# A decoder layer on one core: shift's first sum in quarters, eight groups of columns first, x scaled by GpSimd, the first products in the order of their parts

## The chip, the cores and the metric

The kernel runs on one core of one Trainium2 chip. Its time is device microseconds of one execution. TensorE (PE in the profile) multiplies, and its weight loads (PEld) run beside the products; VectorE (DVE), ScalarE (ACT) and GpSimd (POOL) compute on tiles of 128 partitions; SyncE (SP) issues most of the transfers.

## The reference

One layer of a decoder for 256 positions of width 2048. A conditioning vector c gives shift, scale and gate, and the normalised x is scaled and shifted by them into h. One wide product h W_in feeds two branches, a gated DeltaNet with 32 value heads and an mLSTM with 8 heads. Their outputs are projected, gated, added, projected once more, normalised, and added to x.

```python
shift, scale, gate = jnp.split(jax.nn.silu(c) @ w_ada + b_ada, 3, axis=-1)
h = rms_norm(x, norm_pre_w) * (1.0 + scale[:, None]) + shift[:, None]
proj = h @ w_in
...
merged = jax.nn.sigmoid(gate_a) * y_a + jax.nn.sigmoid(gate_b) * y_b
out = merged @ w_out
return x + gate[:, None] * rms_norm(out, norm_post_w)
```

All inputs are float32.

## The kernel before, in words

**Products in three parts.** Both operands of a product are split into a rounded part and the rest: `split` (L168) makes `hi` with a copy on ScalarE and `lo` = source - hi on VectorE or GpSimd. `mm3` (L221) then issues hi x hi, hi x lo and lo x hi into one PSUM tile. For weights, `prep_w` (L184) splits 1024 columns at a time into `whi` and `wlo`, four buffers each. `split_w` (L174) gives a share of the `wlo` to GpSimd: a counter that starts at -3072 columns and grows by 0.8 of each piece.

**The order of work is written out by hand.** The program is emitted in one order, and each engine works through its own instructions in that order. `Stream` (L63) loads units of weights over SyncE's queue (three buffers of 1 MB), prepares their pieces up to `ahead` pieces before they are used, and uses them. After each used piece `Side.step` (L45) advances the generators of the two branches by one step, up to their next `yield`; `wait(n)` (L605) yields n times. A step is thus the time of one piece.

**How h comes about.** h has 16 chunks of 128 of its 2048 columns (index k). Shift and scale of a chunk are two sums over the 2048 columns of a 1 MB row block of w_ada (`ar`) with silu(c). silu(c) as a row (`crow`) is spread over the 128 partitions by four products of one row into the PSUM tile `csil` (L282). A sum is one VectorE instruction over 2048 columns with an accumulator (L355). x is loaded (`xs`), its squares are summed (L293, L294), the root is taken as a power on GpSimd (`pow_`, L218), `x_scale` (L300) scales two chunks by it on ScalarE, and `x_turn` (L304) transposes them on TensorE and copies them back. `h_chunk` (L327) makes shift `sh` and scale `s1` on ScalarE from the sums, `hf` from both (L333), and splits hf into `h_hi` and `h_lo`.

**The start.** While w_ada comes in, 14 groups of 512 columns of W_in are multiplied in parts: BLOCKS (L340) lists which groups take which chunks k, and between which positions the w_ada units (`ada_units`, L349) are put among them. Six groups (EARLY, NE = 6) begin with chunk 0 alone. Each block's result is copied to SBUF (`part`, L413 and L415) or added to it (L411). `jtile` (L215) hands out four PSUM tiles in turn for these products and the transposes of x, so a tile's next user waits until it has been copied.

**Later.** After the start come eight periods of the DeltaNet branch. Each ends in `base_inverse` (L712), which adds `gdn_stage2` (L764) to the generators; stage 2 begins with the products `mp` (L781) on `ycmp` (L752), and after the products `mz` (L816) and their copy into x0 (L817) comes `pa` (L828). In the last period (zg = 7) nothing holds stage 2 back, as L760 does in the others. Then come four mLSTM units, `mlstm(m)` (L1009), whose `v_after` copies two PSUM tiles into `vt` (L1017), then the projections (`py`) and the last product.

## Time and profile before

| What | Value |
|---|---|
| median of 3 runs | 1606.68 us (1604.88 to 1608.56) |
| the profiled execution, its time | 1603.88 us |
| the profiled execution, its span | 1601.9 us |
| HBM read over the span | 354.40 MB |
| transfers, mean over the span | 232 GB/s |

The span runs from the first to the last instruction of the program. In the rows of the timeline the first number is the start in us from the span's start, the second the busy time, then engine, line, operation, and the tiles as out<-in; in brackets stands how long the engine had been idle and what ended it. In the rows of the stretches each engine has its busy us and, in brackets, its instructions. In the groups the numbers after the bar are busy us, mean ns of one instruction, and the engine's idle time before them.

### The profile page before, as it was taken

To read this page: it belongs to the slowest core of one execution; us is meant where nothing else is said; L and a number is where in the kernel's file an instruction comes from. 1 tells how busy PE (TensorE), PEld (TensorE's weight loads), DVE (VectorE), ACT (ScalarE), POOL (GpSimd) and SP (SyncE) were. 2 spreads that over 40 slices of the span, in tenths; PEclk is the share of its full clock that TensorE was granted. 3 is DMA by queue.
4 is the path that set the end of the run, shared out by engine and by line. 5 is a ranking of instruction groups with operands and counts; after the bars stand their busy time and mean duration, and the time that the engine had idled before them with its cause. 6 is when DMAs were issued, how large, how long until landed. Compare 5 with 4: busy or idle time off the path is not lost.

```text
span 1601.9 us, 25461 instructions
## 1 busy us (share of the span) xinstructions
PE 1577.8 (98%) x9844; PEld 1388.1 (87%) x9844; DVE 1150.1 (72%) x1801; ACT 941.0 (59%) x1503; POOL 236.7 (15%) x193
## 2 busy tenths in 40 slices
...
GB/s 375 339 406 335 279 274 195 289 238 191 170 203 175 205 148 204 164 193 169 193 169 195 149 197 176 187 214 247 290 308 305 227 249 284 283 246 244 200 273 113
DMA packets 96261, 372.37 MB, mean 232 GB/s; under 512 B 26262, under 2 KB 46214, under 8 KB 58252
## 3 DMA queue, kind: packets, MB, share of 16 engines
...
HBM read 354.40 MB, written 16.31 MB: 231 GB/s over the span
## 4 chain that ended last, share of the span: by engine, by line
PE 79%; issue 13%; DMA 3%; DVE 2%; ACT 2%; POOL 1%; SPq 0%; DVEq 0%; POOLq 0%; ACTq 0%
PE pn L223 35%; PE pt L223 28%; PE py L223 8%; DMA raw<-in_dram 1%; POOL mg L1196 1%; PE psa L223 1%; ACT whi L169 1%; DVE wlo L170 1%; DMA ya<-o_dr 1%; DMA ar<-in_dram 1%; PE mz L816 0%; PE mq L807 0%; PE pa L828 0%; PE po L856 0%; PE po L857 0%
## 5 line engine op out<-in xcount | busy, mean ns | idle before, releaser
L170 DVE TENSOR_TENSOR wlo<-raw,whi 128x1024 fp32r<-128x1024 f32 x454 | 561.5, 1245 | 253.9 <-ACT whi L169 248.8
L169 ACT CAST whi<-raw 128x1024 fp32r<-128x1024 f32 (+1 forms) x517 | 533.0, 1046 | 327.1 <-PE pn L223 148.1
L223 PE MATMUL pt<-h_hi,whi 128*128 128x256 f32 x1280 | 367.8, 287 | 0.0
L223 PE MATMUL pt<-h_hi,wlo 128*128 128x256 f32 x1280 | 362.0, 283 | 0.0
L223 PE MATMUL pt<-h_lo,whi 128*128 128x256 f32 x1280 | 362.0, 283 | 0.0
L223 PE MATMUL pn<-whi,h_hi 128*128 128x512 f32 x896 | 353.9, 395 | 6.6 <-ACT whi L169 5.7
L223 PE MATMUL pn<-wlo,h_hi 128*128 128x512 f32 x896 | 350.0, 391 | 1.1 <-POOL wlo L170 0.6
L223 PE MATMUL pn<-whi,h_lo 128*128 128x512 f32 x896 | 349.8, 390 | 0.0
L223 PEld LDWEIGHTS pt<-h_hi,whi 128*128 128x128 f32 x1280 | 245.3, 192 | 1.4
L223 PEld LDWEIGHTS pt<-h_lo,whi 128*128 128x128 f32 x1280 | 245.4, 192 | 0.3
L223 PEld LDWEIGHTS pt<-h_hi,wlo 128*128 128x128 f32 x1280 | 245.2, 192 | 0.0
L223 PEld LDWEIGHTS pn<-whi,h_hi 128*128 128x128 f32 x896 | 168.8, 188 | 42.5 <-ACT whi L169 6.1
L223 PEld LDWEIGHTS pn<-wlo,h_hi 128*128 128x128 f32 x896 | 168.8, 188 | 36.0 <-DVE wlo L170 1.3
L223 PEld LDWEIGHTS pn<-whi,h_lo 128*128 128x128 f32 x896 | 168.6, 188 | 35.3
L170 POOL TENSOR_TENSOR wlo<-raw,whi 128x1024 fp32r<-128x1024 f32 (+1 forms) x63 | 146.3, 2332 | 67.1 <-ACT whi L169 64.9
L223 PE MATMUL py<-whi,yhi 128*128 128x512 f32 x384 | 150.6, 392 | 0.7 <-ACT vt L1017 0.7
L223 PE MATMUL py<-whi,ylo 128*128 128x512 f32 x384 | 149.6, 390 | 0.0
L223 PE MATMUL py<-wlo,yhi 128*128 128x512 f32 x384 | 149.4, 389 | 0.0
L411 DVE TENSOR_TENSOR part<-pn,part 128x512 f32<-128x512 f32 x112 | 73.7, 685 | 52.6 <-PE pn L223 52.6
L169 ACT CAST yhi<-ya 128x512 fp32r<-128x512 f32 x48 | 29.9, 622 | 130.9 <-PE py L223 127.4
L170 DVE TENSOR_TENSOR ylo<-ya,yhi 128x512 fp32r<-128x512 f32 x48 | 33.2, 692 | 86.7 <-ACT yhi L169 78.7
L593 DVE SCALAR_TENSOR_TENSOR qs<-pt,gcv,qs 128x255 f32<-128x255 f32 (+2 forms) x192 | 92.2, 480 | 4.6
...
## 6 DMA issues: line engine op xcount, KB each, us to landing
raw<-in_dram SPq DMA_DIRECT2D x259, 1024.0 KB
ar<-in_dram SPq DMA_DIRECT2D x32, 1024.0 KB
...
```

What stands on the lines that cost most here:

```text
L169: A.copy(hi, src)
L170: (eng or V).tensor_tensor(lo, src, hi.bitcast(F32), op=ALU.subtract)
L223: T.matmul(ps, l, r, start=start and i == 0, stop=stop and i == 2, skip_group_check=True)
L411: V.tensor_tensor(part[g][:, b], ps[b], part[g][:, b], op=ALU.add)
L593: V.scalar_tensor_tensor(dst[:, n, sh:], src[:, 0:S - sh], taps(n, 3 - sh), dst[:, n, sh:], op0=ALU.mult, op1=ALU.add)
L1196: G.tensor_tensor(mcols(b, hf, cg), mcols(b, hf, cg), s_, op=ALU.add)
```

## The change

- **Loads.** c_row goes out on ScalarE's queue into a buffer of the w_ada ring. The first row block of w_ada (shift of chunk 0) is loaded ahead of x, the second (its scale) behind x in three column parts. The constants `bat`, `npre` and `ident` are loaded over GpSimd's queue. c as a column (`ct`) and its Silu move to the late constants.
- **Chunk 0.** Its sums leave the stream of units. The new `first_chunk` runs in place of the first piece's `prep_w`: shift's sum in four quarters, three of them before the squares of x, scale's sum in three parts, each added into `s1` at once; the mean of the squares is put together on GpSimd. The first `whi` is cast on VectorE. hf is read straight from the PSUM tile of the transposes.
- **keep_busy.** Products of a tile of zeros into the PSUM tile `zps`, three of 512 columns behind csil and two of 256 behind the first transposes.
- **First products.** `use_first` issues the twelve products of the first two groups by part: h_hi x whi, h_lo x whi, h_hi x wlo.
- **Blocks.** Eight groups begin with chunk 0 (NE = 8), with other places for the w_ada units; the stream starts with `ahead` at 1. All copies of b = 1 in the first block are VectorE's.
- **Who does what.** `x_scale` on GpSimd except for the first two chunks; `sh` and `s1` on VectorE; GpSimd's share of `wlo` starts at -1024.
- **Late.** For the last period one more step before stage 2 and one more before pa. In the last mLSTM unit the second copy into `vt` is VectorE's.

```diff
--- before.py
+++ after.py
@@ -169,7 +169,8 @@
         A.copy(hi, src)
         (eng or V).tensor_tensor(lo, src, hi.bitcast(F32), op=ALU.subtract)
 
-    share = [-3072.0, START_SHARE]
+    share = [-1024.0, START_SHARE]
+    begin = []
 
     def split_w(src, hi, lo):
 
@@ -185,6 +186,9 @@
         n = min(1024, width - h * 1024)
         hi = wp.tile([P, 1024], F32R, name="whi", tag="whi", bufs=4)
         lo = wp.tile([P, 1024], F32R, name="wlo", tag="wlo", bufs=4)
+        if begin:
+            begin.pop()(raw[:, 0:n], hi, lo)
+            return hi, lo
         split_w(raw[:, h * 1024:h * 1024 + n], hi[:, 0:n], lo[:, 0:n])
         return hi, lo
 
@@ -226,9 +230,8 @@
     bp = x0 = y0 = None
 
 
...
@@ -268,76 +271,133 @@
 
     pcs = ExitStack()
     csil = pcs.enter_context(tc.tile_pool(name="pcs", bufs=1, space=PSUM)).tile([P, D], F32, name="csil")
-    crow = [part[4 + i].rearrange("p b c -> p (b c)")[0:1] for i in range(2)]
-    for i in range(2):
-        SP.dma_start(crow[i], c_row[:, i * 1024:(i + 1) * 1024])
+
...
+    crow = ada_tile()[0:1]
+    A.dma_start(crow, c_row)
+    ar0, ar1 = load_ada(w_ada[0]), ada_tile()
     for b in range(2):
         SP.dma_start(xs[:, b], x[b * P:(b + 1) * P])
-    SP.dma_start(ident, consts[:, 0:128])
-    bat = const("bat", b_ada_t, [P, 32])
-    npre = const("npre", npre_t, [P, KC])
+    bat = cp.tile([P, 32], F32, name="bat")
+    npre = cp.tile([P, KC], F32, name="npre")
+    for t, src in ((bat, b_ada_t), (npre, npre_t), (ident, consts[:, 0:128])):
+        G.dma_start(t, src)
+    parts1 = (slice(0, 1024), slice(1024, 1536), slice(1536, D))
+    for c in parts1:
+        SP.dma_start(ar1[:, c], w_ada[1][:, c])
     for i in range(2):
-        A.activation(crow[i], crow[i], AF.Silu)
+        A.activation(crow[:, i * 1024:(i + 1) * 1024], crow[:, i * 1024:(i + 1) * 1024], AF.Silu)
     for q in range(4):
-        T.matmul(csil[:, q * 512:(q + 1) * 512], one_row, crow[q // 2][:, (q % 2) * 512:(q % 2 + 1) * 512],
-                 start=True, stop=True)
+        T.matmul(csil[:, q * 512:(q + 1) * 512], one_row, crow[:, q * 512:(q + 1) * 512], start=True, stop=True)
+    zero = part[-1][:, 0]
+    G.memset(zero, 0.0)
+    zps = jtile("zps")
+
+    def keep_busy(n, cols=512):
+
+        for _ in range(n):
+            T.matmul(zps[:, 0:cols], zero[:, 0:P], zero[:, 0:cols], start=True, stop=True)
+
     late_c = {}
+
+    def silu_c():
+        yield
+        yield
+        A.activation(sil, ct, AF.Silu)
 
     def late_consts():
         SP.dma_start(con[:, 128:512], consts[:, 128:512])
+        SP.dma_start(ct, c_t)
+        side.add(silu_c())
         late_c.update(gcv=const("gcv", gconv, [P, 256]), mcv=const("mcv", mconv, [P, 64]),
                       abb=const("abb", ab_bias, [P, 1]), alog=const("alog", a_log, [32, 1]),
                       gnw=const("gnw", gnorm, [P, 1]), mnw=const("mnw", mnorm_t, [P, KC]))
 
-    for b in range(2):
-        A.activation(part[2].rearrange("p b c -> p (b c)"), xs[:, b, 0:1024], AF.Square, accum_out=ss[:, b, 0:1])
-        V.scalar_tensor_tensor(part[3].rearrange("p b c -> p (b c)"), xs[:, b, 1024:D], 1.0, xs[:, b, 1024:D],
-                               op0=ALU.mult, op1=ALU.mult, accum_out=ss[:, b, 1:2])
-    V.tensor_reduce(rs, ss, axis=AX.X, op=ALU.add)
-    V.tensor_scalar(rs, rs, 1.0 / D, EPS, op0=ALU.mult, op1=ALU.add)
-    pow_(rs, rs, mhalf[:, 0:2])
-
     def x_scale(k):
         for b in range(2):
-            A.activation(xs[:, b, k * P:(k + 2) * P], xs[:, b, k * P:(k + 2) * P], AF.Copy, scale=rs[:, b:b + 1])
+            v = xs[:, b, k * P:(k + 2) * P]
+            if k:
+                G.tensor_scalar(v, v, rs[:, b:b + 1], None, op0=ALU.mult)
+            else:
+                A.activation(v, v, AF.Copy, scale=rs[:, b:b + 1])
 
     def x_turn(k):
+
         ps = jtile("xps")
         for b in range(2):
             for kk in range(2):
                 T.transpose(ps[:, (b * 2 + kk) * P:(b * 2 + kk + 1) * P], xs[:, b, (k + kk) * P:(k + kk + 1) * P],
                             ident)
-        A.copy(xs[:, :, k * P:(k + 2) * P], ps.rearrange("p (b c) -> p b c", b=2))
-
-
-    for k in range(0, 8, 2):
-        x_scale(k)
-        if k in (2, 4):
-            x_turn(k - 2)
+        if k:
+            A.copy(xs[:, :, k * P:(k + 2) * P], ps.rearrange("p (b c) -> p b c", b=2))
+        return ps.rearrange("p (b k t) -> p b k t", b=2, k=2)
 
 
     bnp = sp.tile([P, KC], F32, name="bnp")
-    V.scalar_tensor_tensor(bnp, bat[:, KC:2 * KC], 1.0, npre, op0=ALU.add, op1=ALU.mult)
...
+    adh = sp.tile([P, 8], F32, name="adh")
+
+    def ada_sum(raw, cols, out):
+        V.scalar_tensor_tensor(raw[:, cols], raw[:, cols], 1.0, csil[:, cols], op0=ALU.mult, op1=ALU.mult,
+                               accum_out=out)
+
+    def first_chunk(src, hi, lo):
+
+
+        def square(b, i):
+            v, junk = xs[:, b, i * 1024:(i + 1) * 1024], part[2 + i].rearrange("p b c -> p (b c)")
+            if i:
+                V.scalar_tensor_tensor(junk, v, 1.0, v, op0=ALU.mult, op1=ALU.mult, accum_out=ss[:, b, i:i + 1])
+            else:
+                A.activation(junk, v, AF.Square, accum_out=ss[:, b, i:i + 1])
+        keep_busy(3)
+        for i in range(4):
+            if i == 3:
+                square(0, 0)
+                square(0, 1)
+            ada_sum(ar0, slice(i * 512, (i + 1) * 512), adh[:, i:i + 1])
+        square(1, 0)
+        square(1, 1)
+        G.tensor_tensor(rs, ss[:, :, 0], ss[:, :, 1], op=ALU.add)
+        G.tensor_scalar(rs, rs, 1.0 / D, EPS, op0=ALU.mult, op1=ALU.add)
+        pow_(rs, rs, mhalf[:, 0:2])
+        V.tensor_reduce(ad[:, 0:1], adh[:, 0:4], axis=AX.X, op=ALU.add)
+        A.activation(sh[:, 0:1], ad[:, 0:1], AF.Identity, bias=bat[:, 0:1])
+        V.scalar_tensor_tensor(bnp, bat[:, KC:2 * KC], 1.0, npre, op0=ALU.add, op1=ALU.mult)
+        for i, c in enumerate(parts1):
+            ada_sum(ar1, c, adh[:, 4 + i:5 + i])
+            V.scalar_tensor_tensor(s1[:, 0:1], adh[:, 4 + i:5 + i], npre[:, 0:1], s1[:, 0:1] if i else bnp[:, 0:1],
+                                   op0=ALU.mult, op1=ALU.add)
+        x_scale(0)
+        xps = x_turn(0)
+        keep_busy(2, 256)
+        hf = sp.tile([P, S], F32, name="hf", tag="hf", bufs=2)
+        A.activation(hf.rearrange("p (b t) -> p b t", b=2), xps[:, :, 0], AF.Identity, bias=sh[:, 0:1],
+                     scale=s1[:, 0:1])
+        V.tensor_copy(hi, src)
+        split(hf, h_hi[:, 0], h_lo[:, 0], V)
+        V.tensor_tensor(lo, src, hi.bitcast(F32), op=ALU.subtract)
+        A.copy(xs[:, :, P:2 * P], xps[:, :, 1])
+        x_scale(2)
+    begin.append(first_chunk)
 
     def h_chunk(k):
 
-        A.activation(sh[:, k:k + 1], ad[:, k:k + 1], AF.Identity, bias=bat[:, k:k + 1])
-        A.activation(s1[:, k:k + 1], ad[:, KC + k:KC + k + 1], AF.Identity, bias=bnp[:, k:k + 1],
-                     scale=npre[:, k:k + 1])
         hf = sp.tile([P, S], F32, name="hf", tag="hf", bufs=2)
         A.activation(hf.rearrange("p (b t) -> p b t", b=2), xs[:, :, k * P:(k + 1) * P], AF.Identity, bias=sh[:, k:k + 1], scale=s1[:, k:k + 1])
-        split(hf, h_hi[:, k], h_lo[:, k], V if k < 2 else G)
-
-    stream = Stream(load_w, side, 2)
-    NG, NE = len(START), 6
+        split(hf, h_hi[:, k], h_lo[:, k], V if k in (1, KC - 1) else G)
+
+    stream = Stream(load_w, side, 1)
+    NG, NE = len(START), 8
     EARLY, REST, ALL = range(NE), range(NE, NG), range(NG)
 
-    BLOCKS = ((EARLY, 0, 1, 1.1, 3.5), (REST, 0, 2, 4, 8), (EARLY, 1, 3, 8, 12), (REST, 2, 2, 12, 16.5),
+    BLOCKS = ((EARLY, 0, 1, 1.1, 2.8), (REST, 0, 2, 3.5, 8), (EARLY, 1, 3, 8, 13.5), (REST, 2, 2, 13.5, 16.5),
               (ALL, 4, 4, 16.5, 26), (ALL, 8, 4, 26, 32), (ALL, 12, 4, 32, 32))
     due = []
 
@@ -349,11 +409,16 @@
     def ada_units():
 
         adders = []
-        for k in range(KC):
+        for k in range(1, KC):
             for pt in range(2):
                 def prep(h, raw, k=k, pt=pt):
                     V.scalar_tensor_tensor(raw, raw, 1.0, csil, op0=ALU.mult, op1=ALU.mult,
                                            accum_out=ad[:, pt * KC + k:pt * KC + k + 1])
+                    if pt:
+                        V.scalar_tensor_tensor(s1[:, k:k + 1], ad[:, KC + k:KC + k + 1], npre[:, k:k + 1],
+                                               bnp[:, k:k + 1], op0=ALU.mult, op1=ALU.add)
+                    else:
+                        V.tensor_tensor(sh[:, k:k + 1], ad[:, k:k + 1], bat[:, k:k + 1], op=ALU.add)
                     j = 2 * (2 * k + pt) - 4
                     if 4 <= j < 16:
                         x_turn(j)
@@ -362,9 +427,7 @@
                     h_chunks(k - 1)
                     if pt == 1:
                         due.append(k)
-                        if k == 0:
-                            h_chunks(0)
-                        elif k == KC - 1:
+                        if k == KC - 1:
                             banks_open()
                     return ()
                 adders.append(lambda i=2 * k + pt, prep=prep:
@@ -405,11 +468,22 @@
                 mm3(ps[b], h_hi[:, k, b * P:(b + 1) * P], h_lo[:, k, b * P:(b + 1) * P],
                     hi[:, o:o + 512], lo[:, o:o + 512], c == 0, c == nk - 1)
 
+        def use_first(hi, lo):
+
+            pss = [[jtile(f"pn{i}") for i in range(2)] for _ in range(2)]
+            for i, (l, r) in enumerate(((h_hi, hi), (h_lo, hi), (h_hi, lo))):
+                for g in range(2):
+                    for b in range(2):
+                        T.matmul(pss[g][b], l[:, 0, b * P:(b + 1) * P], r[:, g * 512:(g + 1) * 512],
+                                 start=i == 0, stop=i == 2, skip_group_check=True)
+            for g in range(2):
+                after(g, pss[g])
+
         def after(g, ps):
             for b in range(2):
                 if k0:
                     V.tensor_tensor(part[g][:, b], ps[b], part[g][:, b], op=ALU.add)
-                elif bi or g < 4 or b == 0:
+                elif bi or b == 0:
                     A.copy(part[g][:, b], ps[b])
                 else:
                     V.tensor_copy(part[g][:, b], ps[b])
@@ -438,6 +512,10 @@
             st_ = {}
 
             def use_piece(h, hi, lo, g=g, st_=st_):
+                stream.ahead = 3 if bi else 1
+                if bi == 0 and g == 0:
+                    use_first(hi, lo)
+                    return
                 for i in range(min(2, per * nk - 2 * h)):
                     gg, c = g + (2 * h + i) // nk, (2 * h + i) % nk
                     if c == 0:
@@ -447,7 +525,10 @@
                         after(gg, st_["ps"])
                     if bi == 0 and gg == NE - 2:
                         h_chunks(1)
-                stream.ahead = 3 if bi else 1
+                    if bi == 0 and gg == 3:
+                        x_turn(2)
+                    elif gg == (NE - 1, NE)[min(bi, 1)] and c == 0 and bi < 2:
+                        x_scale(4 + 2 * bi)
             src = tuple(w_in[START[g + i]][:, k0 * 512:(k0 + nk) * 512] for i in range(per))
             adders.append(lambda src=src, use_piece=use_piece:
                           stream.add(src, lambda h, raw: prep_w(h, raw, per * nk * 512), use_piece,
@@ -532,15 +613,15 @@
         stream.add(w_ab, prep_w, use, after=lambda: side.add(gates(st_["ps"])))
 
     ada = ada_units()
-    ia = 0
+    ia = 2
     for bi, (groups, k0, nk, first, last) in enumerate(BLOCKS):
         if bi == len(BLOCKS) - 1:
             add_ab()
         fs = add_start_groups(bi)
         for j, f in enumerate(fs):
             ahead = first + (last - first) * j / len(fs)
-            while ia < len(ada) and ia < ahead:
-                ada[ia]()
+            while ia - 2 < len(ada) and ia < ahead:
+                ada[ia - 2]()
                 ia += 1
             f()
 
@@ -756,7 +837,7 @@
             if q < 2:
                 V.tensor_copy(y0[c, :, c], ycmp[c])
         res.update(xcmp=xcmp, ycmp=ycmp)
-        yield
+        yield from wait(1 + zg // 7)
         while zg < 7 and side.t < res["t"] + STAGE2_STEPS - 1:
             yield
         side.add(gdn_stage2(zg, res, zr), 0)
@@ -816,7 +897,7 @@
             T.matmul(psz[0:64, m * 64:(m + 1) * 64], p2[64:128, m], x0[64:128, m, 64:128], start=True, stop=True)
         A.copy(x0[0:64, :, 64:128], psz[0:64].rearrange("p (m i) -> p m i", m=8))
         gfree(psz)
-        yield
+        yield from wait(1 + zg // 7)
 
         rr = res["rr"].rearrange("p b z (h d) -> p b (z h d)", h=2)
         ys = bp.tile([P, 2, 512], F32, name="ys", tag="ys", bufs=1)
@@ -1014,7 +1095,11 @@
             for b in range(2):
-                A.copy(vt[:, b, :, 0:S], pv[b].rearrange("p (h d) -> p h d", h=2))
+                src = pv[b].rearrange("p (h d) -> p h d", h=2)
+                if m == 3 and b:
+                    V.tensor_copy(vt[:, b, :, 0:S], src)
+                else:
+                    A.copy(vt[:, b, :, 0:S], src)
             r["vt"] = vt
             if m:
                 side.add(gated())
```

13 lines of the change are left out of this document (7 added, 6 removed).

## The prediction

> **What bounds the kernel now.** I read the page's busy times first, then the waits of TensorE in two stretches, then the busy time by stretch, and only then the timeline of the first 40 us and two places late in the kernel.
>
> ```profile
> span 1601.9 us, 25461 instructions
> ...
> PE 1577.8 (98%) x9844; PEld 1388.1 (87%) x9844; DVE 1150.1 (72%) x1801; ACT 941.0 (59%) x1503; POOL 236.7 (15%) x193
> ```
>
> TensorE is busy for 98% of the span. Nothing in the diff takes product work away, so the change can only win where TensorE stands still or runs slowly. The waits say where it stands (window 0 to 160, then from 160 on):
>
> ```profile
> PE pn L223 <- ACT whi L169: 5.7, 1, 5.7
> ```
>
> ```profile
> PE mp L781 <- DVE ycmp L752: 1.9, 1, 1.9
> PE py L223 <- ACT vt L1017: 0.7, 1, 0.7
> PE pa L828 <- ACT x L817: 0.5, 1, 0.5
> ```
>
> So there is the start, with its long wait before the first product, and three single waits near the end, of 3.1 us together, each of which the diff touches. The stretches of the start:
>
> ```profile
> core 0: us, PE busy (x) PEld busy (x) DVE busy (x) ACT busy (x) POOL busy (x), PEclk, DMA share, GB/s
> ...
> 10.00:20.00 10.00, 3.04 (x10) 1.32 (x8) 5.95 (x11) 7.36 (x18) 0.71 (x1) 1.00 1.01 410
> ...
> 30.00:40.00 10.00, 9.37 (x44) 7.14 (x43) 7.89 (x8) 9.71 (x19) 4.23 (x2) 1.00 1.02 413
> 40.00:50.00 10.00, 9.43 (x44) 7.19 (x43) 3.88 (x5) 9.94 (x20) 8.50 (x5) 1.00 1.01 407
> ...
> 80.00:100.00 20.00, 19.67 (x87) 16.00 (x86) 19.98 (x23) 11.74 (x19) 15.15 (x10) 1.00 1.02 417
> ```
>
> From 30 to 50 us TensorE idles 0.63 + 0.57 us while ScalarE is full, and from 80 to 100 us it idles 0.33 us while VectorE is full: 1.5 us of small stops after the first product.
>
> **The start, as it is.** The timeline of the first 12 us, then from 11 us on:
>
> ```profile
> 1.82 0.83 SPq L275 DMA_DIRECT2D xs<-in_dram  x2
> ...
> 3.88 7.19 PE L282 MATMUL csil<-part,one_row 1*128 1x512 f32 x8 [3.88 <-ACT part L280]
> ...
> 6.68 1.23 DVE L294 SCALAR_TENSOR_TENSOR part<-xs 128x1024 f32<-128x1024 f32 x1 [5.46 <-DMA xs<-in_dram]
> ...
> 9.27 1.23 DVE L294 SCALAR_TENSOR_TENSOR part<-xs 128x1024 f32<-128x1024 f32 x1 [1.36 <-DMA xs<-in_dram]
> ...
> 10.62 0.16 DVE L296 TENSOR_REDUCE rsx<-ssx 128x2 f32<-128x4 f32 x1
> ```
>
> ```profile
> 10.89 0.18 DVE L320 SCALAR_TENSOR_TENSOR bnp<-bat,npre 128x16 f32<-128x16 f32 x1
> 11.06 0.71 POOL L219 TENSOR_TENSOR rsx<-rsx,mhalf 128x2 f32<-128x2 f32 x1 [10.62 <-DVE bnp L320]
> 11.81 1.71 ACT L302 ACTIVATE xs<-xs,rsx 128x256 f32<-128x256 f32 x4 [1.40 <-POOL rsx L219]
> ...
> 12.37 1.97 PE L308 MATMUL xps<-con,xs 128*128 128x128 f32 x8 [1.30 <-ACT xs L302]
> ...
> 12.80 2.29 DVE L355 SCALAR_TENSOR_TENSOR ar<-ar,csil 128x2048 f32<-128x2048 f32 x1 [1.73 <-DMA ar<-in_dram]
> ...
> 15.22 2.29 DVE L355 SCALAR_TENSOR_TENSOR ar<-ar,csil 128x2048 f32<-128x2048 f32 x1
> ...
> 17.97 0.60 ACT L333 ACTIVATE hf<-xs,sh,s 128x256 f32<-128x256 f32 x1
> 18.60 0.40 ACT L169 CAST h_hi<-hf 128x256 fp32r<-128x256 f32 x1
> ...
> 20.00 0.80 PE L223 MATMUL pn<-whi,h_hi 128*128 128x512 f32 x1 [5.67 <-ACT whi L169]
> ...
> 24.42 0.63 PE L223 MATMUL pn<-whi,h_lo 128*128 128x512 f32 x1
> ...
> 24.84 0.45 PE L223 MATMUL pn<-whi,h_hi 128*128 128x512 f32 x1
> ...
> 25.13 0.39 PE L223 MATMUL pn<-wlo,h_hi 128*128 128x512 f32 x1
> 25.36 0.39 PE L223 MATMUL pn<-whi,h_lo 128*128 128x512 f32 x1
> ```
>
> The two row loads of w_ada land at 12.80 and about 15.2, the two sums are done at 17.5, scale and shift, hf, h_hi and the cast of the first weights follow, and the first product starts at 20.00. Products then start every 0.43 us until 24.84 and every 0.23 us after it (25.13 to 25.36). Nine products took 4.84 us where full rate needs 9 x 0.226 = 2.04: 2.8 us lost, 0.47 of it a wait for wlo.
>
> **The change at the start.** The order of the loads is now w_ada[0], x, w_ada[1], weights. A row load is 1 MB; x's two blocks, issued together from 1.82, could be read at 6.68 and 9.27, so one load costs 2.6 us of the queue. In the first one's place stands w_ada[0], issued a microsecond sooner, at about 5.7. x follows at 8.3 and 10.9 and w_ada[1] at 13.5. The three constants between x and w_ada moved to GpSimd's queue, of which this trace has no DMA. They are issued within the first 3 us or so, ahead of GpSimd's memset of zeros and its x steps; from x's 9.27 to the first sum's 12.80 lie 3.5 us, 0.9 more than one load, so by sharing the engines they cost the loads between nothing and 1 us. VectorE wants the first of them at 13.6 (bnp), so they are covered unless they land 10 us after their issue. c_row goes out first, from ScalarE's queue, beside the table load that stands there anyway, so I let csil start 0.3 us sooner than 3.88; its quarters end every 1.7 us, the third at about 9.0. c_t and its Silu move to the late constants, 8 KB and one small step, at nothing.
>
> After that VectorE sets the pace, in its own order. The same form takes 1.23 for 1024 columns and 2.29 for 2048, so 0.70 for 512; from one L355 to the next lie 2.42 us, 0.13 over its length. So a quarter costs 0.83 and a half 1.36. Third quarter 9.0 to 9.8; square of x 11.2; fourth quarter 12.0; second square 13.4; reduce and bnp (0.16 and 0.18) 13.8; w_ada[1]'s half 15.2, its small scale step (0.2, as bnp) 15.4, quarter 16.2, step 16.4, quarter 17.2, step 17.4. Then hf 0.60 and h_hi 0.40 on ScalarE, with what lies between: 18.4. The cast of the first weights moves to VectorE and lies beside hf: 0.75 by its nearest row below (1.2 if it ran at the rate of L294; then it is done at 18.6).
>
> ```profile
> L1087 DVE TENSOR_SCALAR gacc<-raw,sil 128x1024 f32<-128x1024 f32 x2 | 1.4, 746 | 0.0
> ...
> L640 POOL TENSOR_TENSOR b<-gb,ngt 128x2 f32<-128x2 f32 x16 | 5.7, 354 | 0.0
> ...
> L170 POOL TENSOR_TENSOR wlo<-raw,whi 128x1024 fp32r<-128x1024 f32 x58 | 139.7, 2415 | 66.5 <-ACT whi L169 64.3 <-PE pn L223 2.2
> ```
>
> The other branch is shorter: the second square at 13.4, two small GpSimd steps of 0.35, the power 0.71 and the first scaling 0.9 (two of the four in 1.71) give 15.8, four transposes (half of 1.97) 16.8 against 17.4. It has 0.6 us to spare. **First product: 18.4 instead of 20.00, 1.6 us won**; the bounds are 17.4 (csil earlier, no gaps) and 20 (no gain).
>
> *Clock.* keep_busy puts three pairs of 512-column products behind csil and two pairs of 256 behind the transposes. If that lifts the rate before 18.4, and the first products no longer want wlo second, the 2.8 us are won. Against it stands this row: eight csil products in 7.19 us, 0.85 apart. The same kind of plain float32 product late in the kernel:
>
> ```profile
> 542.47 2.87 PE pt L223 x24
> 545.33 0.89 PE pa L828 x8
> ```
>
> Eight of 128 columns in 0.89 are 0.111 each, 0.44 for 512 columns; csil ran at half of that to its end. So 7 us of work with one row of the array did not raise the rate. keep_busy uses all 128 rows, and the first real products needed 4.84 us to raise it; 5.1 us of keep_busy (6 x 0.85) from 10.7 on should do. I take it as working, at 7 in 10; if not, it costs 1.5 us, the rest being covered by VectorE below. The Trainium skill, "TensorE: Matmul & The Clock Gate", Part 1, says that the clock doubles after a busy window of about 3.4 us of any matmul work and falls after an idle one; this trace contradicts it for one-row work. By the page the sum stands as it is, by csil's row it is 1.5 us smaller, which is in the first rival.
>
> *VectorE behind the first product.* Until the ninth group needs the second part of h, VectorE has to do: h_lo 0.4, three wlo of 1.23, seven copies of PSUM of 0.69, two sums of 2.42 and four small steps of 0.2. Together 14.6 us, from 18.4 to 33.0. TensorE has 54 products and one turn of x in that time, 54 x 0.226 + 0.5 = 12.7. It therefore waits 1.9 us, since a PSUM buffer is not free until its copy is done. The fourth piece's wlo is on GpSimd, 2.4 us after its whi: 0.5 more. I put 2.4 us against the change; bounds 0 and 4. The rows of wlo and of such a copy:
>
> ```profile
> 19.98 2.36 DVE L170 TENSOR_TENSOR wlo<-raw,whi 128x1024 fp32r<-128x1024 f32 x2 [0.52 <-ACT whi L169]
> ...
> 31.21 0.69 DVE L415 COPY part<-pn 128x512 f32<-128x512 f32 x1
> ```
>
> One turn of x more lies inside the stream: 0.5 us lost. The scaling of x by GpSimd and sh and s1 on VectorE take some 0.9 us per pair of chunks and 0.7 per chunk from a ScalarE that is full from 30 to 50 us; of the 1.5 us of small stops I let 1.0 go. **Start: 1.6 + 2.8 - 0.5 - 2.4 + 1.0 = 2.5 us.**
>
> **The three late edits.** The last DeltaNet group's second stage now starts a step later. A step is one piece of weights, 24 products, 2.87 us by the row above; ycmp was 1.9 us late, so that wait goes. The same holds for the step after mz and pa's 0.5. What comes next has its weights ready. 2.4 us won.
>
> The third edit moves vt's second copy to VectorE:
>
> ```profile
> 1236.02 1.05 ACT L169 CAST whi<-raw 128x1024 fp32r<-128x1024 f32 x1
> 1236.97 1.06 ACT L1017 COPY vt<-pn 128x512 f32<-128x512 f32 x2
> ```
>
> ```profile
> 1236.32 0.68 DVE L170 TENSOR_TENSOR ylo<-ya,yhi 128x512 fp32r<-128x512 f32 x1
> 1237.09 1.23 DVE L170 TENSOR_TENSOR wlo<-raw,whi 128x1024 fp32r<-128x1024 f32 x1
> ```
>
> TensorE waits for a bank that the first copy (half of 1.06, done at 1237.5) frees, and that copy stays where it is. The second one now stands behind wlo on VectorE: from 1238.3 to 1239.0, where ScalarE had it done at 1238.03 and TensorE wants it three products after its restart, at about 1238.2. So the 0.7 stays and up to 0.7 comes on top; I take 0.6 lost, bounds a gain of 0.7 and a loss of 0.7. **Late edits: 2.4 - 0.6 = 1.8 us.**
>
> **Sum.** 2.5 + 1.8 = 4.3 us. The profiled execution took 1603.88 us (span 1601.9), 2.8 below the median of 1606.68; it becomes 1599.6, and the median 1602.4. A difference of 0.2%, 3.2 us, is about what a measurement of this kernel can tell from no change.
>
> **Rivals.** (1) VectorE and the clock eat the start: the rate stays low for the first products (1.5) and the waits reach 4 instead of 2.4. Then the start gives -0.6 and the whole 1.2 us: 1605.5. For it speaks csil's rate; against it that keep_busy fills the array. Chance 0.20. (2) VectorE's queue does not hold TensorE, because the copies fall between the sums: 2.4 come back, the remaining 0.5 of small stops too, and vt costs nothing: 4.3 + 3.5 = 7.8 us, 1598.9. For it speaks that VectorE idles 6.1 of the 10 us from 40 to 50. Chance 0.20. (3) The late steps gain nothing, since a piece's weights or another side step then come late in their place: 4.3 - 2.4 = 1.9 us, 1604.8. Chance 0.08. (4) Slower: VectorE becomes the bound far beyond the start. It gains 15 x 2 small steps of 0.17 and six copies of 0.69 and loses two wlo to GpSimd: 5.1 + 4.1 - 2.5 = 6.7 us, and it was full from 80 to 100 us already. If all of it shows, the sum is 4.3 - 6.7, 2.4 us slower, 1609.1, and with the low rate 3.9 slower. It decides from the point where VectorE has no idle slice left between 20 and 120 us; against it, it idled 2.1 of 10 us from 30 to 40 and 6.1 of the next 10. Chance 0.08.
>
> **How the numbers follow.** The forecast has 0.44. It and rival 2 lie beyond 0.2% faster but for 0.03 at the forecast's lower end, and 0.02 of rival 3 may: 0.63. Rivals 1 and 3, that 0.03 and half of rival 4 lie within 0.2%: 0.33. Half of rival 4 is 0.04 slower. The range goes from rival 2 with csil's early end, 1597.0, to just past rival 1, 1606.0; the forecast's own is 1600.5 to 1604.
>
> **What would show it.** First product at 18.4 with 0.23 us steps from the start; if at 0.43, keep_busy failed. VectorE without gaps from 9 to 33 us and TensorE stops at PSUM copies between 22 and 33. The rows for mp and pa gone from the waits; py still there, with VectorE's vt copy as its releaser. A first product after 20 us, or a new wait over 1 us after 300 us, makes the forecast wrong.

## The result, and the profile after

| What | before | after |
|---|---|---|
| median of 5 runs each, one after the other on a chip | 1606.68 us | 1617.26 us (1616.96 to 1620.01) |
| ratio to before, 95% interval | | 1.0075 [1.0059, 1.009] |
| profiled execution: its time, its span | 1603.88, 1601.9 us | 1616.96, 1614.8 us |
| first product of the weights | 20.00 us | 20.17 us |
| first product `pab`, at the end of the start | 257.2 us | 265.8 us |
| from there to the end of the span | 1344.7 us | 1349.0 us |

The kernel became 10.6 us slower where 4.3 us faster were forecast; the time lies outside the range of 1597 to 1606 us. Of the span's 12.9 us, 8.7 were lost before `pab` and 4.2 behind it. The page's head, and TensorE's waits up to 160 us and then from 160 us on (us in total, times, the longest):

```profile
span 1614.8 us, 25481 instructions
...
PE 1586.6 (98%) x9854; PEld 1392.4 (86%) x9854; DVE 1183.2 (73%) x1851; ACT 922.7 (57%) x1451; POOL 258.0 (16%) x214
```

```profile
PE xps L336 <- POOL xs L327: 3.7, 4, 2.5
PE pn L227 <- POOL wlo L170: 2.6, 2, 1.5
PE xps L336 <- DMA raw<-in_dram: 2.3, 1, 2.3
PE pn L227 <- DVE part L485: 1.9, 2, 1.6
```

```profile
PE mz L897 <- ACT p L890: 2.7, 1, 2.7
PE py L227 <- DVE vt L1100: 1.6, 1, 1.6
PE py L227 <- ACT vt L1102: 0.9, 1, 0.9
```

The one long wait ahead of the first product is gone from the list only because products of zeros fill it: the first product itself comes 0.17 us later. `mp` and `pa` are gone too. In their places stand waits that were not there: turns of x for GpSimd's scaling, products for VectorE's additions, `mz`, and `py` for VectorE's copy; the wait for GpSimd's `wlo` grew from 0.6 to 2.6 us. (The 2.3 us put down to a DMA lie between two rows of zero products, ahead of the first product.) The stretches:

```profile
10.00:20.00 10.00, 7.67 (x16) 3.48 (x14) 8.63 (x24) 3.49 (x9) 2.94 (x5) 0.89 1.01 376
20.00:30.00 10.00, 10.00 (x43) 7.57 (x41) 8.85 (x11) 7.04 (x12) 1.15 (x1) 0.94 0.70 227
30.00:40.00 10.00, 6.77 (x28) 4.58 (x27) 9.40 (x10) 5.47 (x10) 6.80 (x5) 1.00 1.02 419
40.00:50.00 10.00, 6.93 (x22) 4.80 (x23) 8.01 (x11) 5.61 (x10) 10.00 (x9) 0.66 1.02 414
80.00:100.00 20.00, 18.37 (x81) 14.94 (x80) 19.48 (x20) 9.65 (x12) 16.42 (x10) 1.00 1.02 414
```

In the three stretches where before TensorE idled 0.63, 0.57 and 0.33 us it now idles 3.23, 3.07 and 1.63, 7.9 us instead of 1.5. ScalarE, full from 30 to 50 us before, has room; GpSimd is full from 40 to 50 us. From 40 to 50 us the granted clock is 0.66: 6.8 us at half rate, at which products of 512 columns start 0.43 us apart instead of 0.23.

The rate fell to half in three places of this execution: from 17.8 to 21.2 us, from 41.7 to 48.5 and from 1106.7 to 1110.1. The profile before has no such place ahead of 1598 us. The first of them, as means over 5 us:

```profile
15.00:20.00 5.00, 2.67 (x9) 1.75 (x8) 4.54 (x14) 2.06 (x5) 2.94 (x5) 0.78 1.06 413
20.00:25.00 5.00, 5.00 (x20) 3.65 (x19) 3.98 (x5) 3.29 (x7) 0.00 (x0) 0.88 0.47 154
```

The mean granted clock of the five runs of after is 0.9942, that of fourteen runs of the kernel before 0.9983. The difference, 0.0041 of 1615 us, is worth up to 6.6 us. That is an estimate, and an upper bound, since half rate costs nothing where TensorE would have waited anyway. So a large part of the 10.6 us may be half rate behind the stops and not the stops themselves.

Now the start as the timeline shows it (start, busy time, and in brackets the idle time before and what ended it):

```profile
9.14 1.06 ACT L358 ACTIVATE part<-xs 128x1024 f32<-128x1024 f32 x1 [4.56 <-DMA xs<-in_dram]
...
10.81 4.62 PE L306 MATMUL zps<-part 128*128 128x512 f32 x6
10.92 0.69 DVE L347 SCALAR_TENSOR_TENSOR ar<-ar,csil 128x512 f32<-128x512 f32 x1 [9.68 <-PE csil L298]
...
12.75 0.08 DVE L347 DVE_READ_ACCUMULATOR ar<-ar,csil 128x1 f32 x1
...
18.78 0.22 DVE L375 SCALAR_TENSOR_TENSOR s<-adh,npre,s 128x1 f32<-128x1 f32 x1
...
20.17 1.68 PE L477 MATMUL pn<-whi,h_hi 128*128 128x512 f32 x4
...
21.69 0.63 PE L477 MATMUL pn<-whi,h_lo 128*128 128x512 f32 x2
```

VectorE's first quarter began at 10.92, when the last product of csil was done, though x's first block could be read at 9.14. From there VectorE works without a gap until 19.65: its third quarter is done at 12.83, the last step of scale at 19.00. The first four products start 0.43 us apart, in the first of the three places at half rate, the others from 21.7 us on 0.23 apart. Next, a stop for one of GpSimd's splits, and GpSimd's scaling of x with what stands behind it:

```profile
31.28 0.50 PE L227 MATMUL pn<-wlo,h_hi 128*128 128x512 f32 x1 [1.16 <-POOL wlo L170]
...
38.59 2.36 POOL L170 TENSOR_TENSOR wlo<-raw,whi 128x1024 fp32r<-128x1024 f32 x1 [0.87 <-ACT whi L169]
...
40.94 4.13 POOL L327 TENSOR_SCALAR xs<-xs,rsx 128x256 f32<-128x256 f32 x4
...
41.91 0.69 PE L336 MATMUL xps<-con,xs 128*128 128x128 f32 x2 [2.53 <-POOL xs L327]
...
45.46 0.78 PE L227 MATMUL pn<-whi,h_hi 128*128 128x512 f32 x1
```

Scaling two chunks costs 2.1 us here (four instructions in 4.13) and starts behind a split of 2.4 us in GpSimd's queue. TensorE takes its work in order, so it stands before the turn of x, and when it goes on its products take 0.78 at first: half rate.

The small steps for shift and scale (L421 and L418), as the view of a line lists them (shortest, median and longest in ns), with two of them in the timeline of VectorE and GpSimd's splits of that time:

```profile
L418 DVE SCALAR_TENSOR_TENSOR s<-ad,npre,bnp x15: 220/681/4893, 34.7 to 247.2; 128x1 f32<-128x1 f32 x15
...
L421 DVE TENSOR_TENSOR sh<-ad,bat x15: 260/692/1967, 29.8 to 236.3; 128x1 f32<-128x1 f32 x15
```

```profile
51.59 4.89 DVE L418 SCALAR_TENSOR_TENSOR s<-ad,npre,bnp 128x1 f32<-128x1 f32 x1
...
96.52 1.97 DVE L421 TENSOR_TENSOR sh<-ad,bat 128x1 f32<-128x1 f32 x1
98.41 2.47 DVE L485 TENSOR_TENSOR part<-pn,part 128x512 f32<-128x512 f32 x4
```

```profile
51.69 4.77 POOL L170 TENSOR_TENSOR wlo<-raw,whi 128x1024 fp32r<-128x1024 f32 x2
...
96.09 4.71 POOL L170 TENSOR_TENSOR wlo<-raw,whi 128x1024 fp32r<-128x1024 f32 x2
```

A step on one column lasts 4.89 us and ends within 0.04 us of the end of GpSimd's two splits (51.69 + 4.77 = 56.46); the one at 96.52 ends at 98.49, as GpSimd passes from one split to the next (96.09 + 4.71 / 2 = 98.45). Of the 30 steps 25 last longer than 0.3 us, and each of these ends within 0.04 us of the end of a split on GpSimd. The 30 steps take 32.0 us together. The additions behind the second one free PSUM late, and TensorE stands 1.63 us at 97.

Late, the edits for the last period and for vt:

```profile
1104.15 1.04 ACT L169 CAST whi<-raw 128x1024 fp32r<-128x1024 f32 x1 [6.51 <-DMA raw<-in_dram]
1105.22 0.59 ACT L890 ACTIVATE p<-mq 64x512 f32<-64x512 f32 x1
```

```profile
1105.86 1.31 PE L897 MATMUL mz<-x,p 64*64 64x64 f32 x16 [2.70 <-ACT p L890]
```

```profile
1106.00:1112.00 6.00, 6.00 (x46) 5.88 (x46) 2.90 (x3) 2.94 (x4) 0.00 (x0) 0.72 0.84 315
```

```profile
1249.12 1.22 DVE L170 TENSOR_TENSOR wlo<-raw,whi 128x1024 fp32r<-128x1024 f32 x1
1250.26 0.68 DVE L1100 COPY vt<-pn 128x512 f32<-128x512 f32 x1
...
1251.00 0.50 PE L227 MATMUL py<-whi,yhi 128*128 128x512 f32 x1 [1.59 <-DVE vt L1100]
```

With stage 2 a step later, ScalarE's copy `p` stands behind a cast that waits 6.5 us for its weights, and `mz` waits for that copy; behind the stop lies half rate (0.72 over 6 us). VectorE's copy into vt stands behind a wlo of 1.22 us.

### The profile page after: what moved, and what is told of

Its sections match the earlier page's. It is cut to its first block, busy times and chain, and to the rows that moved or that the text cites. A ratio compares the mean times of both kernels' runs of the same rounds, so it can differ in the third digit from the quotient of the medians.

```text
span 1614.8 us, 25481 instructions
## 1 busy us (share of the span) xinstructions
PE 1586.6 (98%) x9854; PEld 1392.4 (86%) x9854; DVE 1183.2 (73%) x1851; ACT 922.7 (57%) x1451; POOL 258.0 (16%) x214
## 5 line engine op out<-in xcount | busy, mean ns | idle before, releaser
L170 POOL TENSOR_TENSOR wlo<-raw,whi 128x1024 fp32r<-128x1024 f32 (+1 forms) x65 | 150.5, 2324 | 55.9 <-ACT whi L169 55.9
```

The costliest lines, as they stand in the source:

```text
L170: (eng or V).tensor_tensor(lo, src, hi.bitcast(F32), op=ALU.subtract)
```

## The experiments

The times are medians beside runs of the kernel before on the same chip, with the ratio to it and its 95% interval. The start of `pab` and the stops are read from one profiled execution each; the profile of one execution can lie some us off its kernel's median. "What TensorE lost" is the time from the first product of the weights to `pab`, less 1008 products of 0.2267 us and each transpose at 0.1135: before 5.9 us, after 14.0. Of the sixteen profiled executions with keep_busy, eight show the granted clock at half between 17 and 22 us and eight do not. The first twelve products took 3.5 us in after, which has it, and 3.0 in three_undone, which has not; so a difference of 0.5 us in `pab` says little.

| kernel | us | ratio | first product | pab | lost |
|---|---|---|---|---|---|
| after | 1617.26 | 1.0075 [1.0059, 1.009] | 20.17 | 265.8 | 14.0 |
| scale_on_act | 1617.13 | 1.0072 [1.0052, 1.0092] | 20.16 | 262.8 | 11.0 |
| small_one_input | 1615.54 | 1.0063 [1.0043, 1.0083] | 20.18 | 263.2 | 11.3 |
| late_undone | 1612.36 | 1.0046 [1.0029, 1.0062] | 20.40 | 266.4 | 14.3 |
| three_undone | 1607.54 | 1.0014 [1.0005, 1.0023] | 20.16 | 259.2 | 7.4 |
| late_wait_alone | 1610.71 | 1.0028 [1.0018, 1.0038] | 20.21 | 259.8 | 7.9 |
| late_vt_alone | 1609.83 | 1.0027 [1.0015, 1.0039] | 20.40 | 259.8 | 7.7 |
| late_pa_wait_alone | 1606.21 | 1.0008 [0.9999, 1.0018] | 20.16 | 259.1 | 7.3 |
| sums_beside_products | 1607.91 | 1.0016 [1.0006, 1.0025] | 21.04 | 260.4 | 7.6 |
| square_first | 1606.98 | 1.001 [0.9998, 1.0022] | 19.04 | 258.1 | 7.3 |
| splits_on_vectore | 1607.53 | 1.0018 [1.0007, 1.0028] | 20.17 | 260.0 | 8.1 |
| chunk_more_ahead | 1607.21 | 1.0019 [1.0006, 1.0032] | 20.41 | 259.6 | 7.5 |
| six_groups_first | 1609.79 | 1.0029 [1.0018, 1.0041] | 20.16 | 260.9 | 9.1 |
| copies_on_scalare | 1606.67 | 1.0006 [0.9993, 1.0019] | 19.35 | 258.7 | 7.6 |
| two_pieces_ahead | 1608.09 | 1.0012 [1.0002, 1.0022] | 19.23 | 258.9 | 7.9 |
| x_ready_first | 1608.55 | 1.0014 [1.0004, 1.0024] | 20.83 | 261.7 | 9.7 |
| no_zero_products | 1607.76 | 1.0015 [1.0003, 1.0026] | 20.53 | 261.9 | 9.7 |
| zero_products_in_before | 1603.78 | 0.9988 [0.9978, 0.9997] | 19.84 | 255.3 | 4.3 |
| zero_and_pa_wait | 1603.57 | 0.9986 [0.9975, 0.9996] | 20.03 | 257.1 | 5.9 |

**Three causes undone from after, singly and together.**

scale_on_act:

```diff
-            if k:
-                G.tensor_scalar(v, v, rs[:, b:b + 1], None, op0=ALU.mult)
-            else:
-                A.activation(v, v, AF.Copy, scale=rs[:, b:b + 1])
+            A.activation(v, v, AF.Copy, scale=rs[:, b:b + 1])
```

> The changed kernel with all of x scaled by ScalarE again. Theory Q (GpSimd's queue): TensorE's transposes of x wait for GpSimd, which does the scalings of 0.92 us behind whole wlo of 2.4 us; the stop from 39.1 to 45.5 us and the half rate until 48.5 us go, 6.4 + 1.5 us, of which ScalarE's longer list takes back about 1: 6 to 7.5 us faster than the changed kernel, about 1610. Theory L (VectorE's small steps for sh and s1 wait for GpSimd): the stop forms again behind them, 1 to 3 us faster only. Theory B (the order of the groups costs by itself): no difference.

`pab` starts 3.0 us earlier, but the time is within the spread. TensorE's waits for GpSimd's scaling (3.7 us) go, and 1.7 us for ScalarE's scaling come; the 1.9 us for VectorE's additions stay, for VectorE's small steps still take 27.7 us. In the trace the scaling is worth half of what was expected, in the median nothing that shows.

small_one_input (the scale step takes its two scalars from columns, instead of a second input tensor; the shift step likewise):

```diff
-                        V.scalar_tensor_tensor(s1[:, k:k + 1], ad[:, KC + k:KC + k + 1], npre[:, k:k + 1],
-                                               bnp[:, k:k + 1], op0=ALU.mult, op1=ALU.add)
+                        V.tensor_scalar(s1[:, k:k + 1], ad[:, KC + k:KC + k + 1], npre[:, k:k + 1],
+                                        bnp[:, k:k + 1], op0=ALU.mult, op1=ALU.add)
...
-                        V.tensor_tensor(sh[:, k:k + 1], ad[:, k:k + 1], bat[:, k:k + 1], op=ALU.add)
+                        V.tensor_scalar(sh[:, k:k + 1], ad[:, k:k + 1], bat[:, k:k + 1], None, op0=ALU.add)
```

> The changed kernel with sh and s1 still on VectorE, but written with one tensor input and scalars per partition instead of two tensor inputs. Theory L: the 30 small steps, 32.0 us in all where the shortest takes 0.22, end within 0.02 us of GpSimd's running instruction because of their second tensor input; in this form they take about 0.2 us each, 6 us in all, and the stops of TensorE at 97 us (1.8 us) and 104 us (0.5 us) go: 2 to 4 us faster, 1613 to 1615. Theory Q: the big stop at 39 us stays as it is, since the transposes wait for GpSimd. If the small steps wait for something else than the second input, nothing changes.

The same two lines, and the stretch in which TensorE had idled 1.63 us:

```profile
L418 DVE TENSOR_SCALAR s<-ad,npre,bnp x15: 272/273/277, 33.6 to 244.5; 128x1 f32<-128x1 f32 x15
...
L421 DVE TENSOR_SCALAR sh<-ad,bat x15: 214/214/215, 30.0 to 233.7; 128x1 f32<-128x1 f32 x15
```

```profile
80.00:100.00 20.00, 20.00 (x90) 16.56 (x89) 17.72 (x22) 9.55 (x12) 16.42 (x10) 1.00 1.02 416
```

Every step now takes the same 0.21 or 0.27 us, 7.3 us together instead of 32.0, beside the same GpSimd; the stops at 97 and 105 us are gone and `pab` comes 2.7 us earlier; the median is 1.7 us lower, within the spread. The arithmetic and GpSimd's work are unchanged. The kind of instruction changed along with the inputs, from SCALAR_TENSOR_TENSOR and TENSOR_TENSOR to TENSOR_SCALAR; but the 30 sums over 2048 columns in after (L415) are SCALAR_TENSOR_TENSOR too, with their second input `csil` in PSUM, and all of them took 2.27 to 2.29 us among the same splits. So what stretched the steps was their second input from SBUF.

late_undone:

```diff
-        yield from wait(1 + zg // 7)
+        yield
...
-        yield from wait(1 + zg // 7)
+        yield
...
-                if m == 3 and b:
-                    V.tensor_copy(vt[:, b, :, 0:S], src)
-                else:
-                    A.copy(vt[:, b, :, 0:S], src)
+                A.copy(vt[:, b, :, 0:S], src)
```

> The changed kernel with the three late edits undone (both extra steps of the last period and vt's copy on VectorE). My theory: they cost, since p2's copy came to stand behind a whi that waits for its load (mz 2.7 us) and vt's copy behind two wlo (py 1.6 us), 7.1 us of late stops where there were 3.5 before: 3.5 to 4.3 us faster, about 1613.3. Rival: the late stops only follow from the shifted start and come back in another place: no difference beyond 1 us.

4.9 us faster: the late edits together cost that, where 1.8 us were to be won.

three_undone joins the three edits:

> The three edits of the other kernels of this call together. If the causes are separate, the gains add up to 12 to 15 us: 1602 to 1605, at or a little under the kernel before. If the start is bound by VectorE's list anyway, 8 to 10 us: 1607 to 1609.

9.7 us faster than after. In the profiles the scaling and the small steps nearly add up: `pab` comes 3.0 and 2.7 us earlier with one of them mended, 6.6 with both. In the medians the three alone gave 0.1, 1.7 and 4.9 us, 3.0 less than together; with four and five runs each, good to some 2 us, that is hardly resolved. What remains is 0.14% [0.05, 0.23] over before. Its stretches:

```profile
30.00:40.00 10.00, 7.04 (x33) 5.30 (x33) 8.03 (x11) 7.83 (x15) 5.52 (x3) 1.00 1.02 419
40.00:50.00 10.00, 8.28 (x38) 6.02 (x37) 7.43 (x8) 9.68 (x18) 6.30 (x4) 1.00 1.02 414
```

TensorE idles 2.96 and 1.72 us there, still 3.5 us more than before, with ScalarE full again from 40 to 50 us.

**The late edits one by one**, each put back alone into three_undone (the lines of late_undone's diff, the other way).

> The kernel with three edits undone (1607.5 us), with one of the late edits put back: the extra side step before the last group's stage 2. Theory M (that step moves ScalarE's copy of p2 behind a weight cast that waits for its load, so that TensorE's mz product stops for about 2.7 us and then runs at the half rate for some 3 us, while the mp stop of 1.5 us goes): 1609 to 1611 us, an mz row in TensorE's waits, a granted clock below 1 near 1105 us. Rival P (the prediction's own sum: the mp stop goes and nothing comes in its place): 1605.5 to 1606.3 us.

> The kernel with three edits undone (1607.5 us), with one of the late edits put back: the second copy of the last vt on VectorE. Theory M (VectorE's copy stands behind a wlo of 1.2 us, so py waits longer than for ScalarE's second copy): 1608 to 1609.5 us, py waiting for VectorE's vt 1.3 to 1.7 us beside 0.9 us for ScalarE's. Rival P (the prediction's term, 0.6 us gained): 1606.5 to 1607.2 us, with py's waits together below the 1.7 us that they take with both copies on ScalarE.

> The kernel with three edits undone (1.0014 of before), with one of the late edits put back: the extra side step before the last group's pa. Theory M (late steps only move the wait: the edits together cost 4.9 us, of which the wait before stage 2 and vt's copy took 2.2 and 2.0 singly): 0 to 1.5 us slower, 1.0014 to 1.0024 of before. Rival P (the prediction's term): the pa stop of 0.5 us goes and nothing takes its place, 1.001 to 1.0013.

The step before stage 2 costs 0.14% of 1606 us, 2.2 us, although the `mp` stop goes (run against run, ten of each, it is 2.9 us with a 95% interval of 1.5 either way; for vt's copy 2.1 and 1.4). late_wait_alone's ScalarE and TensorE there:

```profile
1095.61 1.04 ACT L169 CAST whi<-raw 128x1024 fp32r<-128x1024 f32 x1 [5.24 <-DMA raw<-in_dram]
1096.68 0.59 ACT L887 ACTIVATE p<-mq 64x512 f32<-64x512 f32 x1
```

```profile
PE mz L894 <- ACT p L887: 1.4, 1, 1.4
```

The `mz` wait has the same cause as in after, and its stop, too, is followed by half rate. vt's copy costs 2.1 us:

```profile
1241.86 1.22 DVE L170 TENSOR_TENSOR wlo<-raw,whi 128x1024 fp32r<-128x1024 f32 x1
...
1243.00 0.68 DVE L1097 COPY vt<-pn 128x512 f32<-128x512 f32 x1
...
1243.73 0.80 PE L227 MATMUL py<-whi,yhi 128*128 128x512 f32 x1 [1.03 <-DVE vt L1097]
```

Behind a first stop of 1.58 us for ScalarE's copy, where three_undone has one of 1.7 and no other, comes one of 1.03 for VectorE's, and then half rate (0.72 from 1243 to 1249 us). The step before pa wins 0.06%, 1 us, not resolved from nothing. Its `pa` wait is gone, but seven profiled executions of kernels without this step (square_first is one) list no `pa` wait either.

**The first product.** Both kernels start from three_undone. sums_beside_products:

```diff
     for q in range(4):
         T.matmul(csil[:, q * 512:(q + 1) * 512], one_row, crow[:, q * 512:(q + 1) * 512], start=True, stop=True)
+        if q == 3:
+            square(0, 0)
+            square(0, 1)
+        ada_sum(ar0, slice(q * 512, (q + 1) * 512), adh[:, q:q + 1])
...
```

> The kernel with three edits undone (1607.5 us), with each quarter of shift's first sum issued right behind its csil product, and the first square ahead of the last quarter. Theory C (VectorE waited for the whole of csil until 10.9 us only because all four products were issued ahead of the first sum): the first quarter starts at 5.6 to 6 us, and the first product of the weights comes at 17.3 to 18.4 us instead of 20.2, so 1605 to 1606 us. Rival D (the dependence is on csil as one tile, wherever the sums are issued): the sums start at 10.9 us or each product waits for the sum before it, and the first product stays at 19.5 us or later, 1607 us or more.

Its VectorE and TensorE:

```profile
6.00 0.69 DVE L300 SCALAR_TENSOR_TENSOR ar<-ar,csil 128x512 f32<-128x512 f32 x1 [4.76 <-PE csil L311]
...
8.86 0.69 DVE L300 SCALAR_TENSOR_TENSOR ar<-ar,csil 128x512 f32<-128x512 f32 x1 [2.16 <-PE csil L311]
```

```profile
6.75 2.07 PE L311 MATMUL csil<-ar,one_row 1*128 1x512 f32 x2 [0.79 <-DVE ar L300]
9.70 2.04 PE L311 MATMUL csil<-ar,one_row 1*128 1x512 f32 x2 [0.88 <-DVE ar L300]
```

The first quarter now starts at 6.00, but each product then waits for the sum before it, and the first product comes later, at 21.04. csil is waited for as one tile: a sum over a part waits for all products issued so far, and a product into a part waits for the sums before it. Rival D holds.

square_first moves `square(0, 0)` and `square(0, 1)` ahead of the quarters:

> The kernel with three edits undone (1607.5 us), with the squares of x's first half ahead of the quarters of shift's first sum, so that VectorE works from 9.2 us while csil is not there. Theory W (the start of the products is VectorE's list without a gap from 10.9 to 19.7 us): the first product of the weights comes 0.8 to 1.1 us earlier, at 19.1 to 19.4 us, and the end 0.5 to 1.1 us earlier, 1606.4 to 1607 us. Rival X (the list is not what ends last, or the loads set the start): the first product moves by less than 0.3 us, or it moves and the stops behind it grow by as much, 1607.2 to 1608 us.

The first product comes at 19.04, 1.1 us earlier, and `pab` too, by 1.1. So VectorE's list does set the first product, and the quarters gain nothing while csil is one tile.

**The stops from 28 to 50 us.** Six edits of three_undone or square_first look for what remains. splits_on_vectore: `share = [-3072.0, START_SHARE]`.

> The kernel with three edits undone (1607.5 us), with the start of the sharing of weight splits put back as before, so that the first splits go to VectorE instead of GpSimd. Theory S (the two stops of 1.3 and 1.7 us at 29 and 33 us come from GpSimd's splits of 2.2 us, and VectorE has room for them): both stops go, 1604.5 to 1606 us. Rival V (VectorE, 1.1 us a split beside sums of 2.3 us, is the bound there): the stops come back under VectorE's name, 1607 us or more.

Rival V came true: two waits for VectorE's wlo (1.4 us) take the place of GpSimd's.

chunk_more_ahead puts c's row into two of part's tiles, and

```diff
-    BLOCKS = ((EARLY, 0, 1, 1.1, 2.8), ...
+    BLOCKS = ((EARLY, 0, 1, 1.6, 3.5), ...
```

> The kernel with three edits undone (1607.5 us, 1.0014 of before), with c's row out of the adaLN ring (in two of part's tiles, as before the change) and the schedule of the first groups asking for one adaLN chunk more ahead of the fourth unit of weights. Theory L (the DMA engines, full in the kernel before, run at 0.42 and 0.90 from 20 to 30 us because the loads that would fill them stand behind the fourth unit, which waits for the first piece's wlo until 21.7 us): the DMA share from 20 to 25 us returns above 0.9 and pab starts 2 to 2.5 us earlier, 1605 to 1605.6 us, 0.9998 to 1.0002 of before. Rival G (the stops from 29 to 46 us are GpSimd's and ScalarE's, not the loads'): pab moves by less than 0.7 us, 1607 us or more.

The DMA share from 20 to 25 us goes from 0.42 to 0.81, from 25 to 30 it falls from 0.90 to 0.69, and `pab` is no earlier (this profile has half rate at the first products, which three_undone's has not): the idle transfers moved and did not go. six_groups_first puts NE, BLOCKS and `Stream(load_w, side, 2)` back:

> The kernel with three edits undone (1607.5 us), with six groups first and two pieces ahead, as before the change. Theory O (the new order takes two groups of one k more ahead of the groups of two, so that the small pieces with their copies and splits crowd ScalarE and GpSimd from 29 to 46 us): the stops there, 6 us together, shrink to 4 us or less, 1604.5 to 1606 us. Rival L (the loads set the start in either order): DMA still idles after 20 us, and the time is within 1 us of 1607.5 us.

The transfers are full again (0.97 and 1.01 from 20 to 30 us), and yet `pab` is 1.7 us later. So idle transfers alone are not the cause.

copies_on_scalare (from square_first, `elif bi or g < 4 or b == 0`) and two_pieces_ahead (from square_first, `ahead` 2 throughout the first block):

> The kernel square_first (three edits undone, squares of x first; 1.001 of before), with the copies of the first four groups' second halves back on ScalarE, as before. Theory V (VectorE is the bound from 20 to 36 us, and the four copies of 0.68 us are what it cannot hold): the stops at 28 and 32 us shrink by 1 to 2.5 us together, pab at 255.5 to 257 us, 0.9995 to 1.0004 of before. Rival A (ScalarE's casts are late as it is, and get later): pab at 257.8 us or later, 1.001 or more.

> The kernel square_first (1.001 of before), with two pieces split ahead of their use from the start on, instead of one. Theory H (the stops at 28 and 32 us, where TensorE waits for a split of 2.4 us that GpSimd begins only 0.9 us ahead of its use, come from the short lookahead): both stops go, pab at 255.5 to 257 us, 0.9995 to 1.0004 of before. Rival A (the splits begin when their casts do, and ScalarE stands behind the copies out of PSUM whatever the lookahead): pab within 0.7 us of 258.1 us, 1.0005 to 1.0015.

Neither brings `pab` forward. x_ready_first (from square_first):

```diff
         for i in range(4):
+            if i == 2:
+                square(1, 0)
+                square(1, 1)
             ada_sum(ar0, slice(i * 512, (i + 1) * 512), adh[:, i:i + 1])
-        square(1, 0)
-        square(1, 1)
...
         pow_(rs, rs, mhalf[:, 0:2])
+        x_scale(0)
+        xps = x_turn(0)
+        x_scale(2)
+        x_turn(2)
+        x_scale(4)
+        x_scale(6)
...
```

> The kernel square_first (1.001 of before), with both pairs of squares ahead of the third quarter, so that the scale of x is there some 2.5 us earlier, and with the first four scalings and the second turn of x ahead of the first product instead of among the products. Theory T (the remaining stops at 36 to 48 us are turns of x that wait for ScalarE's scalings and copies, which the kernel before has behind it by then): the xps waits of 3.3 us fall below 1.5 us, pab at 255.5 to 257 us, 0.9993 to 1.0003 of before. Rival B (ScalarE is only the place where the lateness of the start is seen; the products in front wait for other things then): the xps waits go and others of 1.5 us or more come, pab within 0.8 us of 258.1 us, 1.0005 to 1.0015.

The waits of the turns fall from 3.3 to 1.9 us, but hf now stands behind the four scalings and the first product is at 20.83; other stops come, and half rate with them (0.66 from 35 to 40 us), as rival B has it.

**The clock.** no_zero_products is three_undone without keep_busy.

> The kernel with three edits undone (1607.5 us), without the zero products of keep_busy. Theory K (they lift the granted clock ahead of the first products, and that is worth 1.5 to 2.8 us in the first 16 products): products of 0.43 us until 24 to 26 us, and 1609 to 1610.3 us. Rival L (the loads set the start, so that products done sooner only wait longer): the products are slow, but the stops behind them shrink by as much and the time stays within 1 us, 1606.5 to 1608.5 us.

In its profile the first products run at 0.43 us again and `pab` is 2.7 us later, but the median, 1607.76 us, is that of three_undone within 2 us. Neither theory accounts for both. From `pab` to the end this execution was 2.0 us shorter, with an `mp` stop of 0.2 us instead of 1.4. zero_products_in_before adds three zero products behind the second turn of x, with the clearing of their tile, and nothing else, to the kernel before:

```diff
+    zero = part[-1][:, 0]
+    G.memset(zero, 0.0)
...
+    zps = jtile("zps")
+    for _ in range(3):
+        T.matmul(zps, zero[:, 0:P], zero, start=True, stop=True)
```

> The kernel before, with nothing changed but three zero products behind the second turn of x. Theory K (the prediction's clock term: the first products at 0.23 us instead of 0.43 are worth 2.8 us, and nothing else holds them): pab starts 1.5 to 2.8 us earlier, 0.9983 to 0.999 of before. Rival L (what follows the first products is held by loads and splits anyway): the stops up to 48 us grow by as much, 0.9995 to 1.0005 of before.

```profile
19.84 0.49 PE L223 MATMUL pn<-whi,h_hi 128*128 128x512 f32 x1 [1.62 <-ACT whi L169]
21.10 0.50 PE L223 MATMUL pn<-wlo,h_hi 128*128 128x512 f32 x1 [0.77 <-DVE wlo L170]
21.44 0.40 PE L223 MATMUL pn<-whi,h_lo 128*128 128x512 f32 x1
```

The third product takes 0.40 where it took 0.63 before, `pab` comes 1.8 us earlier, and the kernel is 1.9 us faster, 0.12% [0.03, 0.22]. zero_and_pa_wait adds the step before pa:

> The kernel before with the zero products (0.9988 of before) and the extra side step before the last group's pa (0.5 to 0.6 us by its stop and by its run). Theory (the two gains lie a thousand microseconds apart and add): 0.9982 to 0.9987 of before, 1602.7 to 1603.6 us, without the pa stop of 0.5 us. Rival (in this kernel's late part another wait takes its place, as with the other late edits): 0.9987 to 0.9995.

It is 0.14% [0.04, 0.25] faster than before, and by the two ratios 0.89%, 14 us, faster than after: a version that beats both. It lists no `pa` wait, but neither does zero_products_in_before, and that the step adds to the first gain is not resolved. In its profiled execution the zero products did not help: the granted clock is 0.66 from 20 to 25 us, the products take 0.63, and `pab` starts where it did before.

## Why the prediction was wrong, point by point

- **First product (1.6 us forecast, -0.2 measured).** The step "Third quarter 9.0 to 9.8" failed. It priced each quarter by its own csil product; all four waited for the last one, until 10.92. That VectorE's list sets the first product was right: it ran without a gap, and 1.1 us taken off it moved the first product by 1.1. Its prices were too high: from the end of the third quarter to the last step of scale it took 6.2 us (12.83 to 19.00) where 7.6 were forecast (9.8 to 17.4). So the wait for csil cost 3.0 us, and the prices happened to give 1.4 of them back.
- **Clock (2.8).** The mechanism was right and the size less: alone in the kernel before it moved `pab` by 1.8 us and the time by 1.9 [0.5 to 3.5], and in one of the two profiled executions with it the rate fell back at once. In the changed start TensorE lost 0.9 us between 20 and 26 us where before it had lost 2.9. That the median is the same without the zero products is not explained; that half of the profiled executions with them show half rate around the first product is one candidate.
- **VectorE behind the first product (-2.4) and the small stops (+1.0).** Up to 33 us, where TensorE was to wait 1.9 us for VectorE and 0.5 for GpSimd, it stopped once, 1.16 us for a split on GpSimd. The waits came later: the small stops did not shrink by 1.0 us, they grew by 6.4 in the three stretches shown. The failed term is the price of sh and s1: "four small steps of 0.2", and in rival 4 "15 x 2 small steps of 0.17". They took 32.0 us, 27 more than 30 x 0.17, because of their second SBUF input beside GpSimd's splits. Mended alone, they moved `pab` by 2.7 us.
- **x scaled by GpSimd.** The prediction gave ScalarE's relief as a gain and left out GpSimd's queue, where the scaling stands behind splits of 2.4 us, and TensorE's order, in which nothing passes the turn that waits for it. Mended alone, it moved `pab` by 3.0 us; with the small steps it was 6.6 of the 8.7 us that `pab` came later. In the medians the two were 4.8 us of the 9.7 that three edits gave back, by difference (9.7 less the late edits' 4.9).
- **Half rate behind later stops.** The sum had no term for it: its clock term ends with the first products, and every stop was priced at its length. The profile after has 13.6 us at half rate, and by the mean clock of the runs it was worth up to 6.6 us, the estimate above.
- **Late edits (+1.8 forecast, -4.9 measured).** "What comes next has its weights ready" failed: the next thing was ScalarE's copy p behind a cast whose weights were not there. That is rival 3's mechanism with a price of 2.2 us instead of the lost gain alone. vt's copy behind wlo came as argued, but the price was 2.1 instead of 0.6: a second stop of 1.0 to 1.6 us behind the first, and in late_vt_alone half rate after it. The step before pa is not resolved. Singly the three come to 2.2 + 2.1 - 1.0 = 3.3 us, together to 4.9; the `mz` stop was 1.4 us alone and 2.7 in after.
- **The rivals.** The slower one named VectorE as the bound from 30 to 120 us, which is where TensorE stood, but its 6.7 us of added work would not have been enough; the added time was waiting. The range's lower end, rival 2 with the first product 1.0 us earlier, comes to 1598.9 - 1.0 = 1597.9, not 1597.0.

What stays open: three_undone's `pab` is 2.0 us later than before's, square_first's 0.9. Splits, group order, loads ahead, copies, lookahead and the place of x's scaling were each changed, and none mended it. That they act together is argued, not shown. The mean clock of three_undone's ten runs is 0.9972 against 0.9983, up to 1.8 of the 2.1 us by which its median exceeds that of before; so half rate behind its stops may be most of what remains, which is not shown either.
